# The scan's outputs and z gate with features on partitions, M as the moving operand and the decay factors as rows

## Chip, cores and metric

One NeuronCore of a Trainium2 chip. The metric is the device time of one execution in microseconds; for the kernel before it is the median of three runs.

## What is computed

One layer of a diffusion backbone for 512 latent and 128 context tokens (T = 640, five chunks of 128) and 1024 features, in float32: attention, a gated convolution and a bidirectional state-space scan side by side on one input projection, then a merge and a feed-forward net. The change touches the scan and what reads its result. Cut to that:

```
xs, bm, cm, z            from  h @ w_in  (xs, bm, cm after a convolution over tokens and a SiLU)
acs      = cumsum(dt * a) in a chunk, for 2 directions x 32 heads
cb       = einsum('cign,cjgn->cijg', C, B)                  # 128 x 128 per chunk and group
y_diag   = einsum(cb * exp(acs_i - acs_j) * mask * dt_j, x) # M, per head
y_off    = einsum(C, state before the chunk) * exp(acs)
y        = y_diag + y_off  (forward and backward) + ssd_d * x
y_ssd    = rms_norm(y * silu(z), ssd_norm_g) @ w_ssd_o      # norm over all 2048 features
```

There are 8 groups of 4 heads, 64 features a head, 128 states. Chunks 0 to 3 are latent; chunk 4 is the context and starts from a zero state, so it has no y_off.

## The kernel before, in words

Products of activations with weights take three matmuls each, since both operands are split into a rounded part and a rest (wh/wl, h). Such operands are of a reduced float32 type and stream one column a cycle; the scan's own products are plain float32 and run as two passes, so each of them shows as two matmuls in the trace.

The order of the work is written out by hand. Each engine gets its instructions in the order of the program; a few are marked urgent and put ahead (the weight splits of wload, L163 and L164). The scan (psum(2), two large accumulators "acc" and four single banks "mx") goes group by group. group_scan is a generator that does a step of a group's scan and then yields; between its steps a second generator, group_proj, does the projections of the next group (24 matmuls a part), as many parts as the list PARTS says. In the last group the second generator is a rest of gate projections (spare), three parts a step.

- group_proj: x0, x1, B and C are projected with features on partitions (fparts, fblock, L298: for each weight block two halves of 320 tokens). z is projected with tokens on partitions (tblock, L284 to L286: one token block of 128, all 256 features of the group as moving columns); L870 takes the tanh and L871 forms z(1 + tanh), twice the SiLU.
- Group.turn(c): transposes x0, x1 and B of a chunk (L892), so that tokens are on partitions (xb), and forms x times dt and decay (xw, L897).
- state_of and carry: a chunk's state (L914) and the state before each chunk, for both directions (pv).
- weights(c): reads acs as a row broadcast to all partitions (rw, from D_a, by SP at L927), masks it on GpSimd (L930), takes eight exponentials on ScalarE (L936), and multiplies by C.B (L940, L941): M, tokens j on partitions, tokens i along the free axis.
- outputs(c): C as weights against both directions' states (512 columns, L950), times exp(acs) taken from eas, one factor a token (L952). Then for each head M as weights against 64 columns of x (L956). On VectorE: ssd_d * x (L958), plus M's product (L960), plus both directions (L963), times the z gate (L964). ScalarE squares it and accumulates each token's sum over features (L966).
- turn_back(c), one or more steps later: two transposes by TensorE (L972) and two ScalarE copies that scale by ssd_norm_g (L974) give yF, features on partitions, which SP stores to D_y at the end of the group (L1018).
- After the scan a new set of accumulators is opened (psum(4)); the squares are reduced over groups (L1096) and the norm's factor per token is formed; the last gate projection runs, and load_set later loads D_o, D_c and D_y and splits them for the output projections.

SP is the queue of nearly all transfers: weights (L182), row broadcasts (L927), stores. It works in order and stands while the buffer of its next transfer is still in use.

Of the kernel before, what the change touches and what calls it, by code (L numbers as in the profile page):

```python
# [15 lines left out]
P = 128  # L16
# [70 lines left out]
def layer_kernel(  # L87
# [11 lines left out]
    def nm(s):  # L99
        uid[0] += 1  # L100
        return f"{s}_{uid[0]}"
# [21 lines left out]
    for k, n in (("ab", 48), ("n1", 8), ("n2", 8), ("xcw", 96), ("xcb", 32), ("cw", 24), ("sg", 16)):  # L123
# [4 lines left out]
    dtb, alog, dskip = rws[:, 256:320], rws[:, 320:384], rws[:, 384:416]  # L128
# [7 lines left out]
    ssq = const.tile([P, NT, NG], F32, name="ssq")  # L136
# [4 lines left out]
    D_a = dr.tile([64, T], F32, name="D_a")  # L141
    D_g = dr.tile([3 * KB, P, T], F32, name="D_g")
# [195 lines left out]
    def rstd(sq, parts, tp):  # L338
# [8 lines left out]
        rms_scale(rs, sv, D, tp)  # L347
        return rs
# [95 lines left out]
    eas = const.tile([P, NT, W64], F32, name="eas")  # L444
# [6 lines left out]
    def decays():  # L451
# [55 lines left out]
        act.activation(flat2(eas), acs, AF.Exp)  # L507
# [13 lines left out]
        nc.sync.dma_start(D_a, asb[:W64, :])  # L521

# [323 lines left out]
    with tc.tile_pool(name="ssd", bufs=2) as gp, psum(2):  # L846

        def group_proj(g, out):
            for wsrc, names in ((w_x[g], ("x0", "x1")), (w_bc[g], ("B", "C"))):
                w = wload(wsrc)  # L850
                for m, name in enumerate(names):
                    blk = 2 * g + m if name[0] == "x" else (16 + g if name == "B" else 24 + g)
                    ps = acc()
                    yield from fparts(ps, w, m, 2)
                    xr, t, th = slot(), slot(gp, name), slot()
                    act.copy(v2(xr), hv(ps))
                    act.activation(v2(t), hv(ps), AF.Identity, bias=cw2[:, 96 + blk:97 + blk],
                                   scale=cw2[:, 3 * blk + 1:3 * blk + 2])
# [46 lines left out]
        def group_scan(this):  # L905

            g, b, xb, pv, xw, turn = this.g, this.b, this.xb, this.pv, this.xw, this.turn
            g8 = 8 * g
            ms, ys = {}, {}
# [33 lines left out]

            def outputs(c):
                tok = slice(c * P, (c + 1) * P)
                M = ms.pop(c)
                py = mx()
                if c < 4:
                    pf = mx()
                    pe.matmul(pf, b["C"][:, tok], pv[:, c, :, :], start=True, stop=True)  # L950
                    t = gp.tile([P, 2 * GW], F32, tag="xw", name=nm("yo"), bufs=4)
                    dve.tensor_tensor(heads(t), heads(pf), eas[:, c, g8:g8 + 8].unsqueeze(2).to_broadcast([P, 8, HP]),  # L952
                                      op=mult)
                for r in range(HPG):
                    q = slice(r * HP, (r + 1) * HP)
                    pe.matmul(py[:, q], M[:, r, :], xb[:, c, q], start=True, stop=True)  # L956
                y = ys[c] = gp.tile([P, GW], F32, tag="y", name=nm("y"), bufs=3)
                dve.tensor_tensor(heads(y), heads(xb[:, c, :GW]),  # L958
                                  dskip[:, 4 * g:4 * g + 4].unsqueeze(2).to_broadcast([P, HPG, HP]), op=mult)
                dve.tensor_tensor(y, y, py[:, :GW], op=add)  # L960
# [36 lines left out]
            yF = [slot(gp, "yF") for _ in range(2)]  # L997
# [7 lines left out]
            turn_back(4)  # L1005
# [3 lines left out]
            turn_back(0)  # L1009
# [17 lines left out]
        PARTS = (1, 1, 1, 2, 2, 2, 2, 1, 1)  # L1027
# [30 lines left out]
    def load_op(src, pl, tag="s", raw=None):  # L1058
        if raw is None:
            raw = slot(ph, "raw", bufs=3)  # L1060
            nc.sync.dma_start(raw, src)
        return split_slots(raw, pl, tag=tag)
# [41 lines left out]
    def load_set(i):  # L1104
        src, k0 = sets[i][:2]
        return [load_op(src[k0 + k], *((hpool, "h") if i % 2 else (ph, "s")), raw0.pop(0) if raw0 else None)
                for k in range(KB)]
# [264 lines left out]
def _layout(i):  # L1372
# [20 lines left out]
            a["conv_w"][0].reshape(3, KB, P).transpose(2, 1, 0).reshape(P, 24), _colblk(a["ssd_norm_g"][0])], axis=1),  # L1393
# [3 lines left out]
                                gdr(a["ssd_a_log"][0]).reshape(-1), a["ssd_d"][0]]),  # L1397
# [45 lines left out]
```

## Time and profile before

| | |
|---|---|
| median of 3 runs | 1766.88 us (1764.39 to 1767.08) |
| the profiled execution | 1767.09 us, of which the span of instructions is 1765.2 |
| TensorE busy | 1724.0 us, 98% |
| VectorE busy | 1269.7 us, 72% |
| ScalarE busy | 787.2 us, 45% |
| GpSimd busy | 289.3 us, 16% |
| DMA | 221.76 MB, 126 GB/s in the mean |
| mean granted TensorE clock | 0.994 |

Busy time of TensorE counts matmuls whose ends are modelled and overlap; what one costs in a stream is read from the time between starts. PE is TensorE's matmul, PEld its weight load, which runs beside; DVE is VectorE, ACT ScalarE, SP the queue of transfers. A row of a timeline has the start, the length from the first start to the last end, and the number of instructions that it merges.

### The profile page before, as it was taken

How to read it: one execution, taken by the hardware profiler on the slowest of the kernel's cores; microseconds unless marked ns; L12 is line 12 of the kernel's file. 1: busy time of each engine (PE TensorE's matmuls, PEld its weight loads, DVE VectorE, ACT ScalarE, POOL GpSimd, SP SyncE). 2: the span in 40 equal slices, each digit the busy share in tenths (PEclk: the TensorE clock that was granted, in tenths of full speed). 3: DMA queues.
4: the chain of work that ended last, by engine and by line, in shares of the span. 5: the costliest groups of instructions: out<-in, count | busy, mean ns of one | idle time of the engine just before them, and what ended most of it. 6: DMA issues, size and time to landing. Idle time of an engine off the chain costs nothing.

```text
span 1765.2 us, 30367 instructions
## 1 busy us (share of the span) xinstructions
PE 1724.0 (98%) x11936; PEld 1666.4 (94%) x11936; DVE 1269.7 (72%) x2312; ACT 787.2 (45%) x1588; POOL 289.3 (16%) x249
## 2 busy tenths in 40 slices
PE   7999999999999999999999999999999999999999
PEld 3899999999999999999999999999999999999999
DVE  4599776686646877777777579995578666768685
ACT  4533444465545666566556342222355332424240
POOL 0244441110001111111111000000002131323320
PEclk8999999999999999999999999999999999999999
DMA  7622334211233344334333479873441222223132
GB/s 284 218 87 87 115 117 131 85 50 59 77 110 111 105 138 122 123 111 121 123 123 121 138 263 306 282 231 95 155 144 60 96 61 96 73 84 96 60 93 75
DMA packets 112831, 221.76 MB, mean 126 GB/s; under 512 B 9584, under 2 KB 53488, under 8 KB 111664
## 3 DMA queue, kind: packets, MB, share of 16 engines
q1 hardware_dynamic: 112688, 219.82, 38.5%
q8 instruction: 94, 1.54, 0.3%
q14 instruction: 49, 0.40, 0.1%
HBM read 193.67 MB, written 26.12 MB: 125 GB/s over the span
## 4 chain that ended last, share of the span: by engine, by line
PE 82%; DVE 4%; DMA 2%; issue 1%; ACT 1%; POOL 1%; DVEq 0%; POOLq 0%; ACTq 0%
PE acc L298 32%; PE mx L241 20%; PE mx L298 9%; PE mx L285 3%; PE mx L286 3%; PE mx L284 3%; PE acc L1225 2%; PE mx L956 2%; PE mx L950 2%; DMA out_dram<-so 1%; PE acc L729 1%; PE mx L914 1%; PE acc L745 1%; DVE wl L164 1%; POOL rr L326 1%
## 5 line engine op out<-in xcount | busy, mean ns | idle before, releaser
L298 PE MATMUL acc<-h,wh 128*128 128x320 f32 x1984 | 377.6, 312 | 2.7 <-ACT yF L974 2.0
L163 ACT CAST wh<-wr 128x1024 fp32r<-128x1024 f32 (+2 forms) x226 | 218.8, 971 | 298.9 <-PE acc L298 98.0
L164 DVE TENSOR_TENSOR wl<-wr,wh 128x1024 fp32r<-128x1024 f32 (+2 forms) x226 | 274.2, 1214 | 89.2 <-ACT wh L163 85.7
L298 PEld LDWEIGHTS acc<-h,wh 128*128 128x128 f32 x1984 | 310.3, 189 | 3.3 <-ACT yF L974 2.3
L298 PE MATMUL acc<-h,wl 128*128 128x320 f32 x992 | 228.8, 310 | 0.0
L241 PE MATMUL mx<-h,wh 128*128 128x320 f32 x816 | 183.3, 312 | 4.0 <-DVE g L1279 4.0
L298 PEld LDWEIGHTS acc<-h,wl 128*128 128x128 f32 x992 | 166.8, 188 | 0.0
L284 PE MATMUL mx<-wh,h 128*128 128x256 f32 x560 | 160.2, 286 | 0.0
L286 PE MATMUL mx<-wh,h 128*128 128x256 f32 x560 | 158.5, 283 | 0.0
L285 PE MATMUL mx<-wl,h 128*128 128x256 f32 x560 | 158.4, 283 | 0.0
L298 PE MATMUL acc<-s,wh 128*128 128x320 f32 x768 | 152.7, 309 | 0.0
L241 PEld LDWEIGHTS mx<-h,wh 128*128 128x128 f32 x816 | 138.5, 190 | 4.5 <-DVE g L1279 4.2
L930 POOL TENSOR_SCALAR_AFFINE_SELECT rw<-rw 128x512 f32<-128x512 f32 x80 | 58.0, 749 | 479.0 <-DMA rw<-D_a 308.6
L163 ACT CAST wh<-ws 128x512 fp32r<-128x512 f32 (+1 forms) x102 | 77.2, 762 | 129.2 <-PE mx L241 65.4
L241 PE MATMUL mx<-s,wh 128*128 128x320 f32 x608 | 134.3, 309 | 0.0
L298 PE MATMUL mx<-s,wh 128*128 128x320 f32 x704 | 131.8, 309 | 0.0
L936 ACT ACTIVATE ex<-rw,nlc 128x128 f32<-128x128 f32 x320 | 103.1, 392 | 58.3 <-issue 34.5
L241 PE MATMUL mx<-h,wl 128*128 128x320 f32 x408 | 127.0, 311 | 0.0
L298 PEld LDWEIGHTS acc<-s,wh 128*128 128x128 f32 x768 | 123.0, 188 | 0.3 <-ACT s L166 0.3
L241 PE MATMUL mx<-T,wh 128*128 128x320 f32 x480 | 106.9, 311 | 7.1 <-DVE uv L540 7.1
L298 PEld LDWEIGHTS mx<-s,wh 128*128 128x128 f32 x704 | 110.5, 188 | 0.0
L284 PEld LDWEIGHTS mx<-wh,h 128*128 128x128 f32 x560 | 107.2, 191 | 0.2 <-ACT raw L683 0.2
(298 smaller groups left out, 3653.8 us busy)
## 6 DMA issues: line engine op xcount, KB each, us to landing
wr<-in_w_f_dram SPq DMA_DIRECT2D x64, 512.0 KB, 3.6
rw<-D_a SPq DMA_DIRECT2D x40, 512.0 KB, 3.9
aw<-in_ada_dram SPq DMA_DIRECT2D x64, 256.0 KB, 4.2
wr<-in_w_gt_dram SPq DMA_DIRECT2D x24, 512.0 KB, 4.3
wr<-in_w_cv_dram SPq DMA_DIRECT2D x24, 512.0 KB, 3.8
aw<-in_ada_dram SPq DMA_DIRECT2D x8, 1024.0 KB, 6.8
wr<-in_w_x_dram SPq DMA_DIRECT2D x16, 512.0 KB, 4.5
wr<-in_w_bc_dram SPq DMA_DIRECT2D x16, 512.0 KB, 3.7
```

The lines of the kernel that those rows point to most:

```text
L163: act.copy(hi_t, src)
L164: dve.tensor_tensor(lo_t, src, f32(hi_t), op=sub)
L241: pe.matmul(out, y, z, start=not more and i == 0 and j == 0, stop=i == KB // 2 - 1 and j == 2, skip_group_check=True)
L284: pe.matmul(out, l.hi, r.hi, start=start, stop=False)
L285: pe.matmul(out, l.hi, r.lo, start=False, stop=False)
L286: pe.matmul(out, l.lo, r.hi, start=False, stop=stop)
L298: pe.matmul(bank(ps, e), x, y[:, e * HT:(e + 1) * HT], start=first and i == 0 and j == 0, stop=last and i == k - 1 and j == 2)
L930: pool.affine_select(rw[:, d], rw[:, d], pattern=[[0, HPG], [1 - 2 * d, P]], compare_op=ALU.is_ge, fill=-1e4, base=0, channel_multiplier=2 ...
L936: act.activation(ex[:, d, r, :], rw[:, d, r, :], AF.Exp, bias=nlc[:, c, j:j + 1])
L950: pe.matmul(pf, b["C"][:, tok], pv[:, c, :, :], start=True, stop=True)
L956: pe.matmul(py[:, q], M[:, r, :], xb[:, c, q], start=True, stop=True)
L1225: pe.matmul(ps[:, e, :HT], y, z, start=i == 0 and j == 0, stop=i == KB - 1 and j == 2)
```

## The change

- z is projected like x: features on partitions, two blocks (m) of 128 features, two halves of 320 tokens, in the large accumulators; a group now has four parts of z where it had five, and PARTS loses an entry.
- In outputs the states are the weights (four products of 128 columns) and C is the moving operand; M is the moving operand and 64 columns of x are the weights, so that features come out on partitions: head r lands in the half r % 2 of the partitions and in the columns of r // 2.
- exp(acs) is now wanted as a row for each head: decays stores it in D_e, and decayed(c) reads two broadcasts of four rows, one for each half of the partitions.
- ssd_d becomes a column. turn_back is gone: the gated y is written straight into yF, which is stored after the last output of the group.
- ssd_norm_g is applied when D_y is loaded and split. The sums of squares over features are no longer accumulated by ScalarE: squares() squares yF per group, VectorE adds them up in ssq, and after the scan five matmuls with a column of ones (rstd) sum over partitions.

```diff
-            zs = out["z"] = gp.tile([P, NT, GW], F32, tag="zs", name=nm("zs"))
-            for t in range(NT):
-                pz = mx()
-                tblock(pz[:, :GW], h, t, w)
-                th = gp.tile([P, GW], F32, tag="zt", name=nm("zt"))
-                act.activation(th, pz[:, :GW], AF.Tanh, scale=0.5)
-                dve.scalar_tensor_tensor(zs[:, t, :], th, 1.0, pz[:, :GW], op0=add, op1=mult)
+            zs = out["z"] = gp.tile([P, 2, T], F32, tag="zs", name=nm("zs"))
+            for m in range(2):
+                ps = acc()
+                yield from fparts(ps, w, m, 2)
+                th = slot()
+                act.activation(v2(th), hv(ps), AF.Tanh, scale=0.5)
+                dve.scalar_tensor_tensor(v2(zs[:, m]), v2(th), 1.0, hv(ps), op0=add, op1=mult)
                 yield
...
+            def decayed(c):
+
+                er = gp.tile([P, 2, 2, P], F32, tag="er", name=nm("er"))
+                for e in range(2):
+                    nc.sync.dma_start(er[HP * e:HP * e + HP].rearrange("p d m i -> p (d m) i"),
+                                      D_e[g8 + e:g8 + 8:2, c * P:(c + 1) * P].unsqueeze(0).to_broadcast([HP, 4, P]))
+                return er
...
                 if c < 4:
-                    pf = mx()
-                    pe.matmul(pf, b["C"][:, tok], pv[:, c, :, :], start=True, stop=True)
-                    t = gp.tile([P, 2 * GW], F32, tag="xw", name=nm("yo"), bufs=4)
-                    dve.tensor_tensor(heads(t), heads(pf), eas[:, c, g8:g8 + 8].unsqueeze(2).to_broadcast([P, 8, HP]),
-                                      op=mult)
+                    pf, er = mx(), decayed(c)
+                    for d in range(2):
+                        for m in range(2):
+                            q = 2 * d + m
+                            pe.matmul(pf[:, q * P:(q + 1) * P], pv[:, c, d, m * P:(m + 1) * P], b["C"][:, tok],
+                                      start=True, stop=True)
+                    t = gp.tile([P, 2, 2, P], F32, tag="xw", name=nm("yo"), bufs=4)
+                    dve.tensor_tensor(t, pf.rearrange("p (d m i) -> p d m i", d=2, m=2), er, op=mult)
                 for r in range(HPG):
-                    q = slice(r * HP, (r + 1) * HP)
-                    pe.matmul(py[:, q], M[:, r, :], xb[:, c, q], start=True, stop=True)
...
+                    m, e = divmod(r, 2)
+                    pe.matmul(py[e * HP:(e + 1) * HP, m * P:(m + 1) * P], xb[:, c, r * HP:(r + 1) * HP], M[:, r, :],
+                              start=True, stop=True)
+                y = gp.tile([P, 2, P], F32, tag="y", name=nm("y"))
+                for m in range(2):
+                    dve.scalar_tensor_tensor(y[:, m], b[f"x{m}"][:, tok], dcol[:, 2 * g + m:2 * g + m + 1],
+                                             py[:, m * P:(m + 1) * P], op0=mult, op1=add)
                 if c < 4:
                     for d in range(2):
-                        dve.tensor_tensor(y, y, t[:, d * GW:(d + 1) * GW], op=add)
-                dve.scalar_tensor_tensor(y, y, 0.5, b["z"][:, c, :], op0=mult, op1=mult)
-                jk = gp.tile([P, GW], F32, tag="zt", name=nm("jk"))
-                act.activation(jk, y, AF.Square, accum_out=ssq[:, c, g:g + 1])
-
-            def turn_back(c):
-                y = ys.pop(c)
-                pt = mx()
+                        dve.tensor_tensor(y, y, t[:, d], op=add)
+                dve.scalar_tensor_tensor(yF[:, :, tok], y, 0.5, b["z"][:, :, tok], op0=mult, op1=mult)
+
+            def squares():
                 for m in range(2):
-                    pe.transpose(pt[:, m * P:(m + 1) * P], y[:, m * P:(m + 1) * P], ident)
-                for m in range(2):
-                    act.mul(yF[m][:, c * P:(c + 1) * P], pt[:, m * P:(m + 1) * P],
-                            pv_["sg"][:, 2 * g + m:2 * g + m + 1])
+                    if g + m == 0:
+                        act.activation(ssq, yF[:, m], AF.Square)
+                    else:
+                        q = slot()
+                        act.activation(q, yF[:, m], AF.Square)
+                        dve.tensor_tensor(ssq, ssq, q, op=add)
...
             outputs(2)
-            turn_back(3)
+            nc.sync.dma_start(D_y[2 * g:2 * g + 2].rearrange("m p i -> p m i"), yF)
+            squares()
             yield
-            turn_back(1)
-            yield
-            turn_back(2)
-            for m in range(2):
-                nc.sync.dma_start(D_y[2 * g + m], yF[m])
...
-        PARTS = (1, 1, 1, 2, 2, 2, 2, 1, 1)
+        PARTS = (1, 1, 1, 2, 2, 2, 2, 1)
...
-    s8 = pt2.tile([P, NT], F32, name="s8")
-    dve.tensor_reduce(s8, ssq, op=add, axis=AX.X)
-    r8 = pt2.tile([P, NT], F32, name="r8")
-    rms_scale(r8, s8, 2 * D, pt2)
+    r8 = rstd(ssq, TOKBLKS, pt2, 2 * D)
```

Beside it: decays drops the exponential that filled eas and adds one that fills esb and its store to D_e, and load_set hands load_op the scale of ssd_norm_g for the D_y operands.

## Rows read from the trace of the kernel before

**Rows 1.** The page: busy time, share of the span and instructions of each engine; and the chain that ended last, by engine.
```profile
PE 1724.0 (98%) x11936; PEld 1666.4 (94%) x11936; DVE 1269.7 (72%) x2312; ACT 787.2 (45%) x1588; POOL 289.3 (16%) x249
...
PE 82%; DVE 4%; DMA 2%; issue 1%; ACT 1%; POOL 1%; DVEq 0%; POOLq 0%; ACTq 0%
```

**Rows 2.** Busy time by stage, the stretch of the scan: the stretch, its length, then the busy time (and number) of PE, PEld, DVE, ACT and POOL, the granted clock, DMA share, GB/s.
```profile
555.60:1019.90 464.30, 461.47 (x3215) 431.38 (x3213) 339.24 (x652) 271.78 (x674) 48.90 (x70) 1.00 0.39 121
```

**Rows 3.** The waits of TensorE in the scan's stretch: the waiting line, the releaser, us in total, times, longest.
```profile
PE mx L914 <- DVE xw L897: 2.8, 5, 0.8
```

**Rows 4.** Timeline of TensorE's matmuls, one chunk's output.
```profile
722.00 1.02 PE L950 MATMUL mx<-pv,C 128*128 128x512 f32 x2
722.86 1.00 PE L956 MATMUL mx<-xb,M 128*128 128x64 f32 x8
723.70 0.39 PE L972 MATMUL mx<-cst,y 128*128 128x128 f32 x2
```

**Rows 5.** Timeline of TensorE's matmuls, two other stretches: plain f32 with 64 weight columns and 128 moving ones (a transpose), and with 128 and 128. One matmul's own length is 0.27 us in both.
```profile
225.62 0.71 PE L518 MATMUL acc<-cst,s 128*64 128x128 f32 x5
...
1093.97 1.28 PE L333 MATMUL acc<-cst,r 128*128 128x128 f32 x10
```

**Rows 6.** Groups of matmuls by line and form around the scan (540 to 1025 us): count, busy time, mean ns, idle before.
```profile
L956 PE MATMUL mx<-xb,M 128*128 128x64 f32 x320 | 40.0, 268 | 0.0
...
L972 PE MATMUL mx<-cst,y 128*128 128x128 f32 x80 | 15.3, 274 | 0.0
```

**Rows 7.** Timeline of matmuls (PE) and weight loads (PEld) at two changes of the weights' form: after products with 2 weight columns and 256 moving ones, and before transposes with 64 rows.
```profile
38.62 1.03 PE L405 MATMUL mx<-aw,cf 128*2 128x256 f32 x4
...
39.58 0.52 PEld L413 LDWEIGHTS mx<-comb,ms 4*128 4x128 f32 x4 [0.44 <-issue]
...
101.21 0.31 PE L241 MATMUL mx<-h,wl 128*128 128x320 f32 x1
101.44 0.39 PEld L468 LDWEIGHTS mx<-cst,s 64*128 64x128 f32 x5 [0.19 <-issue]
```

**Rows 8.** Instructions of L346 (the existing row sums): weight loads of 128 and of 64 columns, least, median and greatest length in ns, first and last start in us.
```profile
L346 PEld LDWEIGHTS acc<-cst,s x12: 133/188/192, 1295.8 to 1326.8; 128*128 128x128 f32 x8, 128*64 128x64 f32 x4
```

**Rows 9.** Timeline of TensorE's matmuls: the x projection (six matmuls from the first row to the third), and the first matmul of two token blocks of z and of what follows them.
```profile
699.99 0.75 PE L298 MATMUL acc<-h,wh 128*128 128x320 f32 x4
700.58 0.46 PE L298 MATMUL acc<-h,wl 128*128 128x320 f32 x2
700.87 0.75 PE L298 MATMUL acc<-h,wh 128*128 128x320 f32 x4
...
715.59 0.28 PE L284 MATMUL mx<-wh,h 128*128 128x256 f32 x1
...
721.35 0.38 PE L892 MATMUL mx<-cst,x 128*128 128x128 f32 x2
```

**Rows 10.** Timeline of TensorE's matmuls at the end of the scan.
```profile
1013.80 0.39 PE L972 MATMUL mx<-cst,y 128*128 128x128 f32 x2
...
1019.31 0.60 PE L972 MATMUL mx<-cst,y 128*128 128x128 f32 x4
1021.95 1.44 PE L298 MATMUL acc<-h,wh 128*128 128x320 f32 x4 [2.04 <-ACT yF L974]
...
1025.31 0.76 PE L298 MATMUL acc<-h,wh 128*128 128x320 f32 x4
```

**Rows 11.** Busy time by stage, the stretch behind that stand; columns as in rows 2 (the clock is the third from the right).
```profile
1022.00:1025.30 3.30, 3.30 (x12) 3.30 (x13) 0.00 (x0) 0.00 (x0) 0.00 (x0) 0.50 1.06 329
```

**Rows 12.** Timeline of ScalarE, the same place.
```profile
1020.16 0.70 ACT L529 ACTIVATE s<-acc 128x640 f32<-128x640 f32 x1
```

**Rows 13.** Timeline of VectorE, the same place: the last gate product.
```profile
1015.38 0.42 DVE L964 SCALAR_TENSOR_TENSOR y<-y,zs 128x256 f32<-128x256 f32 x1
```

**Rows 14.** Groups of VectorE by line and form around the scan (540 to 1025 us).
```profile
L871 DVE SCALAR_TENSOR_TENSOR zs<-zt,mx 128x256 f32<-128x256 f32 x40 | 16.7, 418 | 22.3 <-ACT zt L870 22.1
L958 DVE TENSOR_TENSOR y<-xb,rws 128x256 f32<-128x256 f32 x40 | 16.6, 416 | 1.3 <-PE mx L972 1.3
L960 DVE TENSOR_TENSOR y<-y,mx 128x256 f32<-128x256 f32 x40 | 16.5, 412 | 0.6
...
L861 DVE SCALAR_TENSOR_TENSOR x<-s,x 128x640 f32<-128x640 f32 x14 | 11.4, 817 | 0.0
...
L536 DVE SCALAR_TENSOR_TENSOR x<-s,cw,x 128x127 f32<-128x127 f32 x14 | 4.8, 344 | 0.0
```

**Rows 15.** Groups of ScalarE by line and form in the scan's stretch.
```profile
L974 ACT ACTIVATE yF<-mx,par 128x128 f32<-128x128 f32 x76 | 24.4, 365 | 25.7 <-PE mx L972 25.7
...
L966 ACT ACTIVATE jk<-y 128x256 f32<-128x256 f32 x40 | 16.5, 412 | 53.0 <-DVE y L964 53.0
L870 ACT ACTIVATE zt<-mx 128x256 f32<-128x256 f32 x36 | 13.5, 374 | 1.2 <-PE mx L972 0.8
...
L966 ACT ACTIVATION_READ_ACCUMULATOR jk<-y 128x1 f32 x40 | 7.5, 188 | 0.0
```

**Rows 16.** The waits of the queue SP in the scan's stretch, the longest kind.
```profile
SPq L927 <- ACT ex L936: 183.5, 35, 10.2
```

**Rows 17.** The row broadcast's issues: length of the issue in ns (least, median, greatest), and the time from issue to landing in us.
```profile
L927 SPq DMA_DIRECT2D rw<-D_a x40: 370/377/817, 513.6 to 955.5; - x40
...
DMA to landing us min/median/max: 3.7/3.9/7.2
```

More of the change, by code (lines that the diff above doesn't have):

```diff
@@ L122, in layer_kernel @@
     pv_ = {}
-    for k, n in (("ab", 48), ("n1", 8), ("n2", 8), ("xcw", 96), ("xcb", 32), ("cw", 24), ("sg", 16)):
+    for k, n in (("ab", 48), ("n1", 8), ("n2", 8), ("xcw", 96), ("xcb", 32), ("cw", 24), ("sg", 16), ("dc", 16)):
         pv_[k] = par[:, o:o + n]
@@ L127, in layer_kernel @@
     gq, gk = rws[:, 0:128], rws[:, 128:256]
-    dtb, alog, dskip = rws[:, 256:320], rws[:, 320:384], rws[:, 384:416]
+    dtb, alog = rws[:, 256:320], rws[:, 320:384]
     half = const.tile([P, 16], F32, name="half")
@@ L135, in layer_kernel @@
     A2 = const.tile([P, KB, 2], F32, name="A2")
-    ssq = const.tile([P, NT, NG], F32, name="ssq")
+    ssq = const.tile([P, T], F32, name="ssq")
     D_o = dr.tile([NHEAD, P, T], F32, name="D_o")
@@ L141, in layer_kernel @@
     D_a = dr.tile([64, T], F32, name="D_a")
+    D_e = dr.tile([64, T], F32, name="D_e")
     D_g = dr.tile([3 * KB, P, T], F32, name="D_g")
@@ L336, in rowcast, with rstd @@
         return rr
-    def rstd(sq, parts, tp):
+    def rstd(sq, parts, tp, size=D):
         st = acc()
@@ L346, in rstd @@
             pe.matmul(sv[:n, c:c + 1], sq[:, a:a + n], ones[:, 0:1], start=True, stop=True)
-        rms_scale(rs, sv, D, tp)
+        rms_scale(rs, sv, size, tp)
         return rs
@@ L443, in layer_kernel @@
     nlc = const.tile([P, NT, W64], F32, name="nlc")
-    eas = const.tile([P, NT, W64], F32, name="eas")
     dte = const.tile([P, NT, W64], F32, name="dte")
@@ L506, in decays @@
         flat2 = lambda x: x.rearrange("p c n -> p (c n)")
-        act.activation(flat2(eas), acs, AF.Exp)
         act.activation(flat2(cd), tot, AF.Exp)
@@ L521, in decays @@
         nc.sync.dma_start(D_a, asb[:W64, :])
+        esb = slot()
+        act.activation(esb[:W64, :], asb[:W64, :], AF.Exp)
+        nc.sync.dma_start(D_e, esb[:W64, :])
     def gate_proj(br, mt):
@@ L907, in group_scan @@
             g, b, xb, pv, xw, turn = this.g, this.b, this.xb, this.pv, this.xw, this.turn
+            dcol = pv_["dc"]
             g8 = 8 * g
-            ms, ys = {}, {}
+            ms = {}
             def state_of(c):
@@ L957, in outputs @@
[L957 to L960, printed above, removed]
+                    pf, er = mx(), decayed(c)
[4 more added lines that the diff above has]
+                                      start=True, stop=True)
@@ L996, in group_scan @@
             carry(1, 1, ps1)
-            yF = [slot(gp, "yF") for _ in range(2)]
+            yF = gp.tile([P, 2, T], F32, tag="yF", name=nm("yF"))
             outputs(4)
@@ L1004, in group_scan @@
             outputs(3)
-            turn_back(4)
             weights(2)
@@ L1056, in split_slots, with load_op @@
         return split(slot(pl, tag, F32R), slot(pl, tag, F32R), raw, scale)
-    def load_op(src, pl, tag="s", raw=None):
+    def load_op(src, pl, tag="s", raw=None, scale=None):
         if raw is None:
@@ L1061, in load_op @@
             nc.sync.dma_start(raw, src)
-        return split_slots(raw, pl, tag=tag)
+        return split_slots(raw, pl, scale, tag)
     HD2 = D // 2
@@ L1104, in load_set @@
     def load_set(i):
-        src, k0 = sets[i][:2]
-        return [load_op(src[k0 + k], *((hpool, "h") if i % 2 else (ph, "s")), raw0.pop(0) if raw0 else None)
-                for k in range(KB)]
+        src, k0, _, br = sets[i]
+        return [load_op(src[k0 + k], *((hpool, "h") if i % 2 else (ph, "s")), raw0.pop(0) if raw0 else None,
+                        pv_["sg"][:, k0 + k:k0 + k + 1] if br == 2 else None) for k in range(KB)]
     order = [(i, mt) for i in range(2) for mt in range(4)]
@@ L1392, in _layout @@
             xcw.reshape(3, 32, P).transpose(2, 1, 0).reshape(P, 96), _colblk(a["ssd_conv_b"][0]),
-            a["conv_w"][0].reshape(3, KB, P).transpose(2, 1, 0).reshape(P, 24), _colblk(a["ssd_norm_g"][0])], axis=1),
+            a["conv_w"][0].reshape(3, KB, P).transpose(2, 1, 0).reshape(P, 24), _colblk(a["ssd_norm_g"][0]),
+            _colblk(np.repeat(a["ssd_d"][0], HP))], axis=1),
         "ada1": _wt(ada[:, :2 * D].reshape(D, 2, KB, P).transpose(0, 2, 1, 3).reshape(D, 2 * D)),
@@ L1396, in _layout @@
         "rows": np.concatenate([a["q_norm_g"][0], a["k_norm_g"][0], gdr(a["ssd_dt_bias"][0]).reshape(-1),
-                                gdr(a["ssd_a_log"][0]).reshape(-1), a["ssd_d"][0]]),
+                                gdr(a["ssd_a_log"][0]).reshape(-1)]),
         "w_dt": _wt(gdr(sl("dt", 64).reshape(D, 2, 32)).reshape(D, 64), 64)[0],
```

1 line of the change is left out of this document (removed).

## The prediction, made before the changed kernel was run

> **What bounds the kernel now.** I read the busy time and the chain first: TensorE is busy 98% of the span, and the chain that ended last lies on it for 82%, the most of any engine [rows 1]. Then the busy time by stage: the scan's stretch, 555.6 to 1019.9 us, has TensorE busy 461.5 of 464.3 us at the full clock, VectorE 339 and ScalarE 272 [rows 2], and the list of waits gives TensorE in it one kind, 2.8 us in 5 places [rows 3]. So this stage is a queue of matmuls without holes, and an edit is worth what it changes in the time between matmul starts. The other engines count only where they make TensorE wait. The profiled execution took 1767.09 us (span 1765.2 and 1.9 around it), 0.2 above the median 1766.88, so the sum is set against the median.
>
> **Outputs, per chunk.** The timeline of one chunk [rows 4]: the state product (512 columns, plain f32, two passes) starts at 722.00, the M products at 722.86, the turning back at 723.70. So 0.86 us for the state product, 0.84 for the eight matmuls of M (four heads, two passes each), and for the two transposes of a turning back 0.22 (2 x 0.112, the spacing of the x10 in [rows 5]). There are 40 chunk outputs (320/8 and 80/2 [rows 6]); one in five, chunk 4, has no state product, so 32 have.
>
> *Removed: turning back.* 40 x 0.22 = **-8.9 us**. Its ScalarE copies go too.
>
> *State product with the state as weights.* Eight matmuls of 128 columns in place of two of 512: the same columns, four times the weight loads. The near row is the ten f32 matmuls 128x128: (1.28 - 0.275)/9 = 0.112 us from start to start [rows 5]. 8 x 0.112 = 0.90 against 0.86: 32 x 0.04 = **+1.2 us**.
>
> *M as moving operand.* Now each head loads 64 columns of x and streams 128 columns of M, the even heads into the lower half of the result's partitions, the odd ones into the upper half. Five f32 matmuls with 64-column weights and 128 moving columns stand (0.71 - 0.27)/4 = 0.109 us apart [rows 5]; the old ones were held by their 128-column weights. So one slot is 0.109, and the question is how many slots eight matmuls need:
> - eight, if none overlaps: 0.87 against 0.84, 40 x 0.03 = +1.3 us;
> - four, if the two halves of the array always run side by side: 0.44, 40 x -0.40 = -16.2 us;
> - five, if they overlap but start in program order: the order is a a b b a a b b (two passes a head), a pass waits for the one before it on its own half, and the second pass of one head runs beside the first of the next. 5 x 0.109 = 0.55, 40 x -0.295 = **-11.8 us**.
>
> No row has two halves in use in turn. I take five: every spacing in the rows is explained by the columns or the weights of the same half being taken, in the two-column form the weights load while the matmul before streams (spacing 0.215 for 2 x 256 cycles [rows 7], so no load shows), and starts follow program order throughout. That choice carries the sign; both ends stay in the range. The Trainium skill ("TensorEngine Tiling", Key Properties) says that tiles work independently and load and multiply in parallel; by it alone the eight take four slots, which is a rival below, and no run here shows it.
>
> *Entering and leaving the half-width form.* A plain f32 product with 64 weight columns works on a part of the array, and the rows show a hole wherever the part changes. At 39.27 (38.62 + 3 x 0.215) the last two-column matmul starts and streams until 39.48; the next load begins at 39.58, 0.10 later, while elsewhere loads run ahead [rows 7]. At 101.21 a 320-column matmul starts (slots of 0.147, below); the next load begins at 101.44 in place of 101.21, 0.09 after the slot's end [rows 7]. And the first load after a hole is not hidden: 0.11 for 128 columns [rows 5], and 0.055 less for 64 (133 against 188 ns [rows 8]). In and out: 0.10 + 0.055 + 0.10 + 0.11 = 0.365 us, once per output: 40 x 0.365 = **+14.6 us**. Nothing hides it, since TensorE is the bound. Least: 0.30 (+12); most: 0.42 (+17).
>
> **The z gate.** Before: two token blocks of 24 matmuls of 256 columns from 715.59 to 721.35, 0.120 each; 120 a group, 14.40 us. After: the loop of the x projection, six matmuls of 320 columns in 0.88 us (699.99 to 700.87), 0.147 each; 96 a group, 14.08 [rows 9]. The columns are equal; 24 starts go. 8 x -0.32 = **-2.5 us**.
>
> **The end of the scan.** The row norm's sums move from ScalarE's accumulators to TensorE: five f32 products with one moving column, ten matmuls held by their weights, 10 x 0.11 = **+1.1 us** at the head of the last gate projection. Now TensorE ends the last transposes near 1019.9, stands until 1021.95, and runs at half clock (granted 0.50, 1.2 GHz) until 1025.3 [rows 10, 11]; it waits for the banks, whose last readers are a tanh (1020.16 + 0.70 [rows 12]) and the copies of the turning back, which it waits for last [rows 10]. After, the copies are gone, and the next in line is that tanh, or the sum of squares: y is ready about 2.0 us after the last M product as now (1013.80 to 1015.80 [rows 10, 13]), then two squares of 0.70 and two adds of 0.82 with a weight split of 1.2 between them, near +6; TensorE has three parts of 1.76 us in between (to +5.3), the tanh frees the banks near +6.4. So it stands some 1.1 us, not 2.0: **-0.9 us**. The half clock after the stand I leave as it is. Bounds: -2.5 (no fall of the clock) to +1.5 (the sums 2.4 us later).
>
> **What lies beside.** VectorE: 80 products of 128 columns (0.344) replace 40 x (0.416 + 0.412); 16 gate products of 640 (0.82) replace 40 of 0.418; 15 adds of 0.82 are new [rows 14]: 27.5 - 33.1 + 13.1 - 16.7 + 12.3 = +3 us on 339 of 464. ScalarE loses 80 copies (0.365), 40 squares (0.41 + 0.19), 40 tanhs (0.37) and gains 32 operations of 0.70 [rows 12, 15]: -46 us. Both hidden behind TensorE; if not, the wait on xw in [rows 3] would grow first. The next group's first turned x is now used one z part sooner, 7 us (two parts of 24 x 0.147) after it is made instead of 9 and more; a wait there would be of the kind of [rows 3], at most 0.8 us a group. Taking the z gate into the larger banks (two of them, each filled in 7 us and read in 1.5) costs nothing.
> SP: 64 new issues of 128 KB (two for each of 32 outputs), 0.38 us each if they cost what the row broadcast costs, landing in 4 to 7 us [rows 17]. Each stands in the queue behind the row broadcast of its step, which already waits for ScalarE's exponentials, 184 us in all [rows 16]; its own buffer came free two outputs earlier, so it adds no wait there, and it lands an output (464/40, some 11 us) before VectorE wants it. Behind it wait weight loads of later steps. D_y's one store (two before) now stands ahead of the last z part and the next group's first row broadcast, and waits for VectorE's last y, earlier than it used to wait for the copies. D_e: one exponential and one store, 300 us before use. The scale in the split of the D_y operands changes no count. All 0, at most +3.
>
> **Sum.** -8.9 + 1.2 - 11.8 + 14.6 - 2.5 + 1.1 - 0.9 = -8.2 us; with 1 us for a few new waits like those of [rows 3], -7.2: 1766.9 - 7.2 = **1759.7 us**.
>
> **Rivals.**
> - *The halves don't overlap.* Eight slots in place of five: 40 x 0.327 = +13.1, so +5.9: 1772.8, slower. For it: every matmul in the trace starts after the one before has streamed. Against: all those share columns. It decides from about 6.7 slots on. Chance 0.25.
> - *They pair fully.* Four slots: 40 x -0.109 = -4.4, 1755.3. For it: loads of 64 columns take half a slot, so they could keep two halves fed. Against: the two passes of a head stand next to each other in the order, and starts keep the order. The Trainium skill ("TensorE: Matmul & The Clock Gate", Part 3) also says that matmuls start and end in program order, which is against it; no run here shows either. Chance 0.12.
> - *The decay rows come late.* VectorE then stands at the first product of an output, and weight splits and the next outputs queue behind it. From 0.25 us of TensorE wait per output the gain is gone; at 0.3 us x 32 it is +2.4: 1769. Against: the row broadcast, twice as large, runs steps ahead. Chance 0.08.
>
> **How the numbers follow.** Forecast 0.55, own range 1756 to 1764 (switch 0.30 to 0.42, end of the scan). The range takes in full pairing and most of the first rival: 1754 to 1774. About 0.2% (3.5 us) is what a measurement can tell from no change. Faster: 0.55 less a tenth, 0.12, and some of the late rows: 0.63. Slower: most of 0.25 and a part of the late rows: 0.23. Same: 0.14.
>
> **What would show it.** In the changed trace: M's matmuls in pairs with starts that fall together, about 0.55 us for eight (0.87: first rival; 0.44: second); a hole of 0.10 and an unhidden load before and after them; no transposes after outputs; z in 320-column slots of 0.147; TensorE's stand near 1020 shorter, ten one-column matmuls after it. VectorE standing on a transfer from D_e would show the third rival. The prediction fails if the holes are absent or the eight take 0.87.

## The result, and the profile after

The changed kernel takes **1749.56 us** (median of four runs, 1747.73 to 1750.03) against 1765.79 for the kernel before on the same chip: ratio 0.9902 [0.9891, 0.9914], 16.2 us less. The forecast was 1759.7 with a range of 1754 to 1774. The sign was right, the size was not: the time lies below the range, and below the rival of full pairing (1755.3) too. A second set of runs gave 0.9902 again. The profiled execution took 1749.79 us, its span 1748.0.

First the page (answers to rows 1), then the busy time by stage of the stretch in which the scan of before lay (answers to rows 2; columns as there).

```profile
PE 1711.9 (98%) x11866; PEld 1657.2 (95%) x11866; DVE 1278.6 (73%) x2302; ACT 759.8 (43%) x1420; POOL 289.2 (17%) x249
...
555.60:1019.90 464.30, 462.86 (x3257) 436.50 (x3257) 361.09 (x666) 254.47 (x529) 51.54 (x71) 1.00 0.49 149
```

TensorE is the bound as before. What the time went from is read between two marks that both kernels have: the first and the last start of M's products. The row gives count, least, median and greatest length in ns, and these two starts; first the kernel before, then after.

```profile
L956 PE MATMUL mx<-xb,M x320: 217/275/275, 572.1 to 1013.7; 128*128 128x64 f32 x160
```

```profile
L971 PE MATMUL mx<-M,xb x320: 272/273/324, 570.8 to 996.2; 128*64 128x128 f32 x160
```

Before, 441.6 us lie between them, after 425.4: 16.2 us less, as much as the medians differ (the two profiled executions are 17.3 us apart). This length M to M is the yardstick below. (A single matmul's 273 ns is its own length; the cost is the distance of starts.)

Timeline of TensorE's matmuls of one output after the change (answers to rows 4):

```profile
717.82 1.06 PE L965 MATMUL mx<-C,pv 128*128 128x128 f32 x8
718.80 0.66 PE L971 MATMUL mx<-M,xb 128*64 128x128 f32 x8
719.39 0.86 PE L299 MATMUL acc<-h,wh 128*128 128x320 f32 x4
```

M's eight matmuls last 0.66 us in all, one of them 0.27, so from the first start to the last one 0.39. The single records lie in four pairs: 718.802 and 718.809, .962 and .969, 719.071 and .078, .180 and .187. Between the pairs lie a first distance of 0.16, in which the first load shows (0.05), and two of 0.11; with a slot of 0.11 for the last pair that makes 0.44 and the load. That is **four slots**, not five. The hole of the half-width form is there too: the state product's eighth start is at 718.597, so its slot of 0.107 ends at 718.704, and M starts 0.10 later; its last slot ends near 719.296, and the next start is at 719.39, 0.09 later; the projection behind it needs 0.86 for four where 0.75 is usual [rows 9], 0.11 more.

The list of TensorE's waits in the scan (answers to rows 3) holds nothing but the stand at the end, and the wait on xw is gone:

```profile
PE acc L347 <- ACT s L531: 1.4, 1, 1.4
```

The decay rows are no wait for VectorE. Its first product per output (L968), with what it stood for, and the transfers:

```profile
L968 DVE TENSOR_TENSOR yo<-mx,er x32: 675/691/693, 579.9 to 996.0; 128x512 f32<-128x512 f32 x32
...
  PE mx L965: 14.1, 15
```

```profile
L951 SPq DMA_DIRECT2D er<-D_e x64: 579/608/2231, 514.7 to 983.2; - x64
...
DMA to landing us min/median/max: 3.0/4.6/7.6
```

An issue takes 0.61 us, not the 0.38 taken from the row broadcast, and still nobody waits for it.

### The profile page after: what moved, and what is told of

It is laid out like the page before. It is cut to its first block, busy times and chain, and to the rows that moved or that the text cites. A ratio compares the mean times of both kernels' runs of the same rounds, so it can differ in the third digit from the quotient of the medians.

```text
span 1748.0 us, 30158 instructions
## 1 busy us (share of the span) xinstructions
PE 1711.9 (98%) x11866; PEld 1657.2 (95%) x11866; DVE 1278.6 (73%) x2302; ACT 759.8 (43%) x1420; POOL 289.2 (17%) x249
## 4 chain that ended last, share of the span: by engine, by line
PE 88%; DVE 6%; issue 2%; DMA 1%; ACT 1%; POOL 1%; DVEq 0%; SPq 0%; POOLq 0%; ACTq 0%
PE acc L299 41%; PE mx L242 21%; PE mx L299 10%; DVE wl L165 2%; PE mx L965 2%; PE mx L917 2%; PE mx L971 1%; PE acc L731 1%; PE mx L286 1%; PE mx L287 1%; PE mx L285 1%; PE acc L1230 1%; PE mx L406 1%; PE mx L943 1%; PE mx L894 1%
## 5 line engine op out<-in xcount | busy, mean ns | idle before, releaser
L299 PE MATMUL acc<-h,wh 128*128 128x320 f32 x2496 | 475.3, 313 | 0.7 <-ACT s L788 0.5
L299 PEld LDWEIGHTS acc<-h,wh 128*128 128x128 f32 x2496 | 390.1, 188 | 3.8 <-issue 2.7
L299 PE MATMUL acc<-h,wl 128*128 128x320 f32 x1248 | 285.9, 310 | 0.0
L299 PEld LDWEIGHTS acc<-h,wl 128*128 128x128 f32 x1248 | 209.3, 188 | 0.0
L299 PEld LDWEIGHTS mx<-s,wh 128*128 128x128 f32 x704 | 110.5, 188 | 0.0
L165 DVE TENSOR_TENSOR wl<-ws,wh 128x512 fp32r<-128x512 f32 (+1 forms) x102 | 97.1, 952 | 12.6 <-ACT wh L164 11.6
L242 PEld LDWEIGHTS mx<-s,wh 128*128 128x128 f32 x608 | 102.5, 189 | 0.0
L1185 DVE SCALAR_TENSOR_TENSOR s<-mx,mod,s 128x320 f32<-128x320 f32 x144 | 56.1, 433 | 63.0 <-PE mx L299 63.0
L299 PE MATMUL acc<-s,wl 128*128 128x320 f32 x384 | 98.0, 309 | 0.0
```

The lines of the kernel that those rows point to most:

```text
L165: dve.tensor_tensor(lo_t, src, f32(hi_t), op=sub)
L242: pe.matmul(out, y, z, start=not more and i == 0 and j == 0, stop=i == KB // 2 - 1 and j == 2, skip_group_check=True)
L299: pe.matmul(bank(ps, e), x, y[:, e * HT:(e + 1) * HT], start=first and i == 0 and j == 0, stop=last and i == k - 1 and j == 2)
L1185: dve.scalar_tensor_tensor(dst[:, a:a + n], bank(ps, e)[:, a - e * HT:a - e * HT + n], gcol[:, k, s:s + 1], dst[:, a:a + n], op0=mult, op1 ...
```

## The experiments

"Ratio" is to the kernel before, run beside each on the same chip. Two questions: how many slots M takes and what the form's hole costs; and where the waits went.

**The changed kernel again**, unaltered.

> The changed kernel once more, as the yardstick of the three kernels beside it. All theories: ratio to the kernel before 0.989 to 0.992, eight M matmuls per output in four slots of 0.107 us, TensorE without any wait on xw in the scan.

1748.38 us, 0.9902 [0.989, 0.9914]; M to M 425.4 again. The result stands.

**The order of the heads.** In M's loop:

```
-                for r in range(HPG):
+                for r in (0, 2, 1, 3):
```

> The changed kernel with the heads of M's product issued in the order 0, 2, 1, 3, so that neighbours in the program share a half of the array (a a a a b b b b in passes). If the queue only pairs neighbours of different halves, heads 2 and 1 can pair and the rest can't: six slots, 2 x 0.107 x 40 = +8.6 us against the changed kernel. If no pairing were behind the four slots at all, eight slots, +17 us, or no change. If each half runs its own order over the whole queue, four slots and no change (within 1 us).

Still four slots, as the timeline shows; the two of a pair now lie 13 ns apart.

```profile
746.52 0.66 PE L971 MATMUL mx<-M,xb 128*64 128x128 f32 x8
747.11 0.49 PE L943 MATMUL mx<-C,B 128*128 128x128 f32 x2
```

1749.73 us, 0.9905 [0.9891, 0.992], M to M 425.6. With both even heads (four passes on the lower half) ahead of both odd ones, starts in program order allow at most one pair. So it is not neighbours that pair up: each half goes on with its own matmuls while matmuls of the other half that stand earlier in the program have not started. This refutes the step of the prediction that starts follow program order throughout.

**All heads on one half.** The upper half of the features is left with its skip term (the VectorE lines that do this are left out below); the odd heads' products are made and not used.

```
-                    pe.matmul(py[e * HP:(e + 1) * HP, m * P:(m + 1) * P], xb[:, c, r * HP:(r + 1) * HP], M[:, r, :],
+                    pe.matmul(py[:HP, r * P:(r + 1) * P], xb[:, c, r * HP:(r + 1) * HP], M[:, r, :],
...
```

> The changed kernel with all four heads' M products sent to the lower half of the partitions (four column blocks of 128); the odd heads' products are not used and the upper half of y gets only the skip term (two more VectorE operations of 64 partitions per output; values wrong). The form of the weights, the columns and the holes stay, only the second half is never used. Theory (two halves side by side make the four slots): eight slots of 0.109 per output, +4 x 0.109 x 40 = +17.4 us against the changed kernel, near the kernel before. If the speed came from the 64-column weights alone: no change.

```profile
746.27 1.09 PE L971 MATMUL mx<-M,xb 128*64 128x128 f32 x8
```

```profile
L971 PE MATMUL mx<-M,xb x320: 272/273/323, 572.1 to 1014.7; 128*64 128x128 f32 x160
```

Eight slots, 1.09 us in place of 0.66. M to M is 442.6, 17.2 longer, that is 40 x 0.43: four slots of 0.107 an output. Time 1766.79, 1.0004 [0.9995, 1.0014]. The pairing is worth about what the whole change gains, and the first rival (halves that don't overlap) is what this run shows by force.

**The full-width form.** Weights of 128 columns (both heads of a pair), so that no form changes; the odd heads' outputs are then made with the even head's M.

```
-                    pe.matmul(py[e * HP:(e + 1) * HP, m * P:(m + 1) * P], xb[:, c, r * HP:(r + 1) * HP], M[:, r, :],
+                    pe.matmul(py[:, r * P:(r + 1) * P], xb[:, c, m * P:(m + 1) * P], M[:, r, :],
...
-                                             py[:, m * P:(m + 1) * P], op0=mult, op1=add)
+                                             py[:, 2 * m * P:(2 * m + 1) * P], op0=mult, op1=add)
```

> The changed kernel with 128 columns of x (two heads) as the weights of each head's product, so that it runs on the whole array; half of each result is not used, and the odd heads' outputs take the even head's M (values wrong, the same number of operations). No change of form, so no holes, but eight slots of 0.112: 0.90 us per output. Theory of four slots plus two holes (0.43 + 0.36 = 0.79): +0.10 x 40 = +4 us against the changed kernel. If the holes cost nothing: +0.46 x 40 = +18 us. If the holes cost 0.5 or more: no change or faster.

```profile
749.00 1.05 PE L965 MATMUL mx<-C,pv 128*128 128x128 f32 x8
749.89 1.06 PE L971 MATMUL mx<-M,xb 128*128 128x128 f32 x8
750.78 0.39 PE L943 MATMUL mx<-C,B 128*128 128x128 f32 x2
```

```profile
L971 PE MATMUL mx<-M,xb x320: 272/275/275, 571.5 to 1001.6; 128*128 128x128 f32 x160
```

The starts run through without a hole. M to M is 430.1, 4.7 longer; in a group's period, from its first M product to the next group's, 56.44 against 55.89, or 0.11 an output. The eight full-width slots take 0.1075 us each in the mean of a group's starts (4.30 us for 40), so four slots saved (0.43) and the hole paid leave 0.11: the hole is **0.32 us** an output. The run on one half says the same without a count of slots saved, since both take eight: its period is 58.04, and 58.04 - 56.44 = 1.60 us for five outputs, 0.32 each. Time 1753.42, 0.993 [0.9917, 0.9944].

**Two outputs in one step**, so that one pair of form changes a group goes: outputs is rewritten to take several chunks, and makes all state products of chunks 1 and 2, then all their M products. Of the edit, the calls:

```
-            outputs(1)
             yield
-            outputs(2)
+            outputs(1, 2)
```

> The changed kernel with the outputs of chunks 1 and 2 made in one step: both state products, then both M products, so that the half-width form is entered and left four times a group and not five. By the holes of 0.36 us a period is 0.36 us shorter: 55.53 us against 55.89; 8 x 0.36 = -2.9 us. If M's product, four heads more in a row, does not pair as before, or VectorE's later outputs make TensorE wait, no change or slower.

1746.58 us, 0.9889 [0.9872, 0.9906], the lowest median of all, though by the intervals not clear of the changed kernel; its period is 55.55, 0.34 less a group. That is the hole once more, by itself.

**Two such pairs a group** (outputs 0 and 3 as well).

> The same with chunks 0 and 3 in one step as well (and M of chunks 1 and 2 made after that step): period 55.17 us, 8 x 0.72 = -5.7 us against the changed kernel. Against it: four single banks are all in use in such a step, and M's C.B product stands right behind it, so TensorE may wait for VectorE's first product; a wait of 0.7 us a group would take the gain of the second pair back.

```profile
753.77 1.09 PE L975 MATMUL mx<-M,xb 128*64 128x128 f32 x16
```

```profile
PE mx L917 <- DVE xw L899: 1.0, 4, 0.3
```

Sixteen matmuls lie in eight slots (1.09 us for all), but TensorE waits on xw again, and the first six periods are 55.27 (in a group without such a wait) to 55.82; 1747.95 us, 0.9893 [0.9877, 0.9909], not below the version with one pair. The second hole is given back to waits.

**The state's store in a buffer of its own, in the kernel before.** What this tests came from the chain of waits in the kernel before, and from the row of its store of the context state (so):

```profile
734.17 0.60 ACT so L981
734.77 0.02 issue
734.79 5.22 DMA out_dram<-so
740.01 0.02 issue
740.03 0.69 DVE M L938
...
743.70 0.61 DVE xw L897
744.31 0.04 issue
744.35 1.12 PE mx L914 x2
```

```profile
L982 SPq DMA_DIRECT2D out_dram<-so x8: 338/338/914, 561.4 to 970.3; - x8
...
  DVE M L938: 22.2, 8
...
DMA to landing us min/median/max: 2.6/5.0/5.8
```

The store shares its buffers with M. VectorE's next M sum (L938) waits until it has landed, 22.2 us in eight groups, and what stands behind the sum on VectorE includes xw, for which TensorE waits. After the change the store lands in 2.1 us and VectorE waits 4.1:

```profile
L996 SPq DMA_DIRECT2D out_dram<-so x8: 343/344/350, 560.7 to 953.8; - x8
...
  DVE M L941: 4.1, 8
...
DMA to landing us min/median/max: 2.0/2.1/2.9
```

The queue SP around one such store, before and then after:

```profile
731.92 0.33 SPq L182 DMA_DIRECT2D wr<-in_w_z_dram  x1
732.29 0.91 SPq L1018 DMA_DIRECT2D D_y<-yF  x2
733.65 0.33 SPq L182 DMA_DIRECT2D wr<-in_w_x_dram  x1
734.79 0.37 SPq L982 DMA_DIRECT2D out_dram<-so  x1
```

```profile
723.47 0.38 SPq L1024 DMA_DIRECT2D D_y<-yF  x1
725.29 0.33 SPq L183 DMA_DIRECT2D wr<-in_w_x_dram  x1
728.42 0.34 SPq L996 DMA_DIRECT2D out_dram<-so  x1
```

Before, z's weight load, D_y's two stores and x's weight load are issued 2.9, 2.5 and 1.1 us ahead of it, and all four are still under way when it is issued; after, one store is issued 5 us and one load 3.1 us ahead. Over the 112 stores of this kind in all fourteen traces the landing goes with this number: with four transfers under way it took 4.4 to 6.5 us (12 stores, all in the kernel before and in the next one), with two or fewer 2.0 to 4.0 (100 stores). The edit, in the kernel before:

```
-            so = gp.tile([P, 2 * GW], F32, tag="M", name=nm("so"))
+            so = gp.tile([P, 2 * GW], F32, tag="so", name=nm("so"), bufs=1)
```

> The kernel before with a buffer of its own for the final state's copy (so), which shares its buffers with M. Theory: in the kernel before VectorE's next M waits for the landing of so's store (22 us in all), behind it ScalarE's exponentials, the copy of x and xw, and TensorE's waits on xw; with an own buffer these go: faster by about 3.4 us (the four later groups that are 0.5 to 1.0 us longer than the first two become as short), no wait on xw. Rival (the waits come from ScalarE's copies and squares of the turning back): no change.

```profile
L956 PE MATMUL mx<-xb,M x320: 217/275/276, 573.3 to 1011.5; 128*128 128x64 f32 x160
```

```profile
PE acc L298 <- ACT yF L974: 2.0, 1, 2.0
```

The store still lands after 4.9 us in the median, and nobody waits for it: the wait on xw is gone, the first six periods are all 57.57 (before: 57.58 to 58.62), and M to M falls by 3.4 us to 438.2. So the shared buffer was the cause. Over all runs it is less: 1763.2 us, 0.9989 [0.998, 0.9997], or -1.9 us [-3.5, -0.5].

**D_y's store later, in the changed kernel**, to bring the wait back: its line moved behind the group's last yield.

> The changed kernel with the store of yF put back to the end of the group, after the last part of z, where the kernel before had it. Theory: the waits on xw are gone because this store now leaves the queue earlier, so that the store of the final state (so) lands in 2 us and not in 5, and VectorE's M, ScalarE's exponentials and copy of x, and xw follow sooner; put back, so lands in 4 to 5 us again, VectorE waits for it some 20 us in all (4 in the changed kernel), and TensorE's waits on xw return, +1 to +3.4 us. Rival (the waits went because ScalarE lost the copies and squares of the turning back): no change, no waits on xw.

1749.79 us, 0.9908 [0.9894, 0.9922], no wait. Inconclusive: in SP's queue the store still came ahead of the next weight load (721.67 and 723.49, then the state's store at 726.63), so the neighbourhood was not changed, and the state's store still landed in 2.1 us in the median. That the landing is slower because of the transfers under way is an inference: they go together in every trace, but no run moved them alone. The wait itself is shown.

**No turning back, in the kernel before.** The two transposes go, and ScalarE's copies read the outputs as they stand, so that D_y holds them unturned.

```
-                    pe.transpose(pt[:, m * P:(m + 1) * P], y[:, m * P:(m + 1) * P], ident)
...
-                    act.mul(yF[m][:, c * P:(c + 1) * P], pt[:, m * P:(m + 1) * P],
+                    act.mul(yF[m][:, c * P:(c + 1) * P], y[:, m * P:(m + 1) * P],
```

> The kernel before without the 80 transposes of the turning back; the copies read y itself (values wrong, all copies and stores stay). By the rows of before: 40 x 0.224 = -8.9 us. The copies no longer wait for TensorE, so the store of yF comes earlier too; by the theory that its neighbourhood to so's store makes the waits on xw, these go as well: -8.9 - 3.4 = -12.3 us. Rival for the waits: -8.9 us with the waits on xw as they were.

1754.45 us, 0.9941 [0.9926, 0.9956]. The wait on xw goes here too (the store lands in 2.7 us). Against the kernel with the store's own buffer the period falls from 57.57 to 56.62: 8 x 0.95 = 7.6 us for the transposes alone; by the medians of the two it is 8.75.

**z in the new way, in the kernel before.** z is projected as in the change and read in the old shape, so that the gate meets other values.

```
...
+            zt = gp.tile([P, 2, T], F32, tag="zs", name=nm("zs"))
+            out["z"] = zt.rearrange("p m i -> p (m i)").rearrange("p (t q) -> p t q", q=GW)
...
+                yield from fparts(ps, w, m, 2)
...
-        PARTS = (1, 1, 1, 2, 2, 2, 2, 1, 1)
+        PARTS = (1, 1, 1, 2, 2, 2, 2, 1, 0)
```

> The kernel before with only the z gate made with features on partitions in 320-column matmuls; the result is read in the old shape (values wrong). By the spacing of the matmuls 8 x -0.32 = -2.5 us. The parts of z are longer and one fewer, so the waits on xw may move; if the store of yF stays next to so's store they stay: -2.5 us; if they go: -5.9 us.

1760.75 us, 0.9975 [0.9966, 0.9985]: 4.4 us less, and no wait on xw. Against the store's own buffer (1763.2), which has no such wait either, 2.45 us remain for z; the shortest period, 57.27 against 57.57, says 8 x 0.30 = 2.4.

```profile
728.48 0.80 SPq L1019 DMA_DIRECT2D D_y<-yF  x2
729.38 0.40 SPq L182 DMA_DIRECT2D wr<-in_w_x_dram  x1
731.76 0.34 SPq L983 DMA_DIRECT2D out_dram<-so  x1
```

This run also says something of the wait. ScalarE's copies and squares are all there, M and the state's copy still share their buffers, and D_y's two stores stand 3.3 us ahead of the state's store, nearly as in the kernel before. But z's weight load is now issued at 721.87, 9.9 us ahead (9.0 in the changed kernel), at most two transfers are under way, the state's store lands in 2.5 us in the median, and the wait is gone. So D_y's nearness alone does not make the wait, and the z gate alone ends it.

**The row norm's sums later**, behind the last gate projection in place of ahead of it, alone and with the one pair of outputs.

```
-    r8 = rstd(ssq, TOKBLKS, pt2, 2 * D)
...
     run(gate_proj(*SPARE[-1]))
+    r8 = rstd(ssq, TOKBLKS, pt2, 2 * D)
```

> The changed kernel with the norm's sums (ten one-column matmuls) moved behind the last gate projection. Theory: they stand in a stretch at full clock and cost 1.1 us there as before; the stand at the end of the scan stays (1.4 us, for the tanh that frees the banks), but the dense matmuls follow it at once. If the clock falls for the stand alone, no change; if it falls for the stand and the one-column matmuls together, the half clock of some 3 us goes: -1.7 us.

> The changed kernel with both of the edits that won something: chunks 1 and 2 in one step, and the norm's sums behind the last gate projection. If they add: period 55.55 us, no half clock behind the stand, -2.4 and -0.6 to -1.7 us against the changed kernel, 1745 us in the mean, ratio 0.988. If the merged step's later sums of squares hold up the sums or the stand grows (1.9 us with the merged step), -2.4 us alone.

1747.99 us, 0.9896 [0.988, 0.9912], and 1748.24 us, 0.9895 [0.9878, 0.9911]. Neither can be told from its partner without the edit. The half clock after the stand is missing in these two profiles, but it is missing in two others with the sums in the old place as well (the full-width form and the one pair).

## Why the prediction was wrong, step by step

The terms of the sum, us:

| term | predicted | measured | from |
|---|---|---|---|
| turning back | -8.9 | -7.6 | period without it; -8.75 by medians |
| state product | +1.2 | +1.0 | 3.56 against 3.44 us of starts a group |
| M as moving | -11.8 | -16.2 | four slots of 0.109 in place of 0.84, x40 |
| form holes | +14.6 | +12.8 | 40 x 0.32, full-width run |
| z gate | -2.5 | -2.45 | z alone, by medians |
| end of scan and sums | +0.2 | +0.5 | stand 1.45 for 2.04, ten matmuls in 1.13 |
| waits | +1 | -3.4 | the store's own buffer, by the profile; -1.9 by all runs |
| sum | -6.2 (written as -7.2) | -15.3 | the result: -16.2 |

About 1 us is in none of these terms; with the waits by all runs, about 2.4. The first lies inside the groups: without waits a period fell from 57.57 to 55.89, 8 x 1.68 = 13.4 us, of which the terms of a group explain 12.4. Where, the runs do not show.

- **The addition.** The prediction's own terms come to -7.2 us ahead of the new waits and to -6.2 with them, not to -8.2 and -7.2, so its forecast should have read 1760.7, and the times of its rivals 1 us more as well. The slip brought the forecast 1 us nearer to the result by luck; no step of the mechanism hangs on it.
- **The step that failed first: "five, if they overlap but start in program order".** The measured count is four, the bound that the prediction gave a chance of 0.12 as "They pair fully". The reason against it was that the two passes of a head stand next to each other and starts keep the order. The first half of this is true of the program and has no force: the pairs lie 7 ns apart, and with the heads in another order 13 ns apart, so order between the halves costs nothing. 40 x 0.109 = 4.4 us. The forecast's sign needed a pairing of some kind, since the run on one half gained nothing. The Trainium skill ("TensorE: Matmul & The Clock Gate", Part 3) says that matmuls start and end strictly in program order; across the two halves the reordered run doesn't agree, since its third head would have to start before the second. The Trainium skill ("TensorEngine Tiling (Array Packing)", Key Properties) says that tiles work independently and in parallel; the four slots agree.
- **The second: "with 1 us for a few new waits like those of [rows 3]".** The sign was wrong. The existing waits went, 3.4 us by the profile. The prediction read [rows 3] as a price for new waits and never asked what made xw late; the chain of waits led to a store that shares its buffers with M. The runs point to what it counted at nothing, the order of transfers in the queue: it named D_y's store, which "now stands ahead of the last z part", but not z's weight load, and the run with the z gate alone lost the wait with D_y's stores nearly where they were. Which of the transfers must go is not settled, since the run meant to move D_y's store back did not move it past its neighbours.
- **The hole was right in mechanism, 0.32 for 0.365**: 0.10 in, 0.09 out, and the loads that show, 0.05 and 0.11, stand in the timeline; they add to 0.35, the one pair of outputs gives 0.34, and the net of the full-width run is 0.32. Had M not paired, the hole would have made the change worth nothing, as the run on one half shows.
- **Turning back, state product, z** came out as costed, turning back between 0.15 and 1.3 us below its term.
- **The end of the scan**: the wait passed to the tanh as foretold, and the stand is 1.45 us, not 1.1. The timeline:

```profile
1001.52 0.46 PE L299 MATMUL acc<-h,wl 128*128 128x320 f32 x2
1003.43 1.27 PE L347 MATMUL acc<-cst,ssq 128*128 128x1 f32 x10 [1.45 <-ACT s L531]
1004.56 0.83 PE L299 MATMUL acc<-h,wh 128*128 128x320 f32 x4
...
1006.72 1.27 PE L299 MATMUL acc<-h,wh 128*128 128x320 f32 x4
...
1009.70 0.75 PE L299 MATMUL acc<-h,wh 128*128 128x320 f32 x4
```

- **The third rival** (the decay rows come late) is refuted: VectorE's first product waits for TensorE alone.
- **The range** moved one term at a time: its low end is the full-pairing rival less 1.3 us. The two misses, 4.4 us each (2.9 for the waits by all runs), pointed the same way; one of them alone, taken off the forecast of 1759.7, gives 1755.3, inside the range.

## What to carry to other kernels

Where a plain f32 product needs only half of the array's columns, put alternate products on the two halves: here they ran side by side in both orders that were tried, and the gain was half the slots less one hole of 0.32 us for each stay in that form, so gather such products into one stay. Before a change is costed, follow each existing wait of the bound engine back to what released it, since a change that moves a store can end that wait or make it. A buffer that a store reads stays taken until the store has landed, so let it share its place with nothing that is urgent.

## What the runs showed of the hardware

- Matmuls on the two halves of the array do not wait for each other's place in the program: eight passes of 128 moving columns took four slots of 0.107 to 0.109 us with the heads in either order, eight when all were on one half.
- Going into the form with 64 weight columns and out of it again cost 0.35 us by the timeline of one output, 0.34 by the one pair of outputs and 0.32 by the full-width run.
- The clock after the same stand of TensorE differs between executions. The kernel before stood 2.04 us and then ran at 0.50 [rows 10, 11]. With the store in its own buffer TensorE stood 2.04 us at the same place and the clock did not fall, as this row of its timeline (0.86 for four matmuls, where 1.44 stands in rows 10) and of its stages (granted clock 1.00) shows:

```profile
1019.74 0.86 PE L298 MATMUL acc<-h,wh 128*128 128x320 f32 x4 [2.04 <-ACT yF L974]
```

```profile
1019.70:1023.00 3.30, 3.26 (x22) 3.26 (x23) 0.00 (x0) 0.00 (x0) 0.00 (x0) 1.00 1.05 334
```

After the change, 1.45 us of stand were followed, not at once but from 1006.2 on, by a fall (the 1.27 for four matmuls above; this row of its stages has a granted clock of 0.57):

```profile
1006.00:1010.00 4.00, 4.00 (x18) 4.00 (x18) 4.00 (x6) 2.54 (x5) 0.83 (x1) 0.57 0.94 274
```

That half clock lasted 3.4 us in the profiles of the first and second set of runs and 6.8 us with the heads reordered; with the full-width form there was none. Half clock over 3.4 us loses half of that, 1.7 us, and over 6.8 twice as much. That is a part of the few us by which runs of one kernel differ: of 29 runs of the kernel before on one chip, the four with a mean granted clock of 0.992 took 1767.9 us in the mean, the three with 0.996 took 1762.3. It is a reason not to read 1 us from one profile.
